# Writing zeros to hold back two weight transfers in the opening of a hybrid layer

## The chip, the cores and the metric

The kernel runs on one core of a Trainium2 chip. The metric is the device time of one execution in microseconds (us); the figure for a kernel is the median of its runs. Engines are named as in the profile: PE is TensorE (PEld its weight loads), DVE is VectorE, ACT is ScalarE, POOL is GpSimd, SP is SyncE, which only issues transfers here. ACTq and SPq are the instruction queues of ScalarE and SyncE; a row there is the issue of a transfer.

## The reference

One layer (`DEPTH = 1`) of a streaming encoder on 256 tokens of width 2048, in float32:

```python
def reference(x, attn_norm, w_in, b_forget, q_norm, k_norm, out_norm_fox, out_norm_sb,
              w_out, ffn_norm, w_up, conv_w, conv_b, w_down):
    for layer in range(DEPTH):
        h = rms_norm(x, attn_norm[layer])
        x = x + hybrid_mixer(h, w_in[layer], b_forget[layer], q_norm[layer], k_norm[layer],
                             out_norm_fox[layer], out_norm_sb[layer], w_out[layer])
        h = rms_norm(x, ffn_norm[layer])
        x = x + conv_ffn(h, w_up[layer], conv_w[layer], conv_b[layer], w_down[layer])
    return x
```

`hybrid_mixer` projects `h @ w_in` (2048 x 6152), splits the columns into queries, keys and values of eight heads of a softmax attention with forget gates and eight heads of a stick-breaking attention, normalizes each group's output and multiplies by `w_out`. `conv_ffn` projects up to 11264 columns, convolves three tokens per channel, gates with SiLU and projects down. The change touches only the first of all these products: the first 512 columns of `h @ w_in`, which are the queries of four heads.

## The kernel before

Every product is made of three: the weights, which arrive as float32 in a buffer `w_raw`, are split into a rounded part `w_hi` (a cast) and the rest `w_lo` (a subtraction), and the activations likewise into the two parts of `hT`. TensorE multiplies hi by hi, lo by hi and hi by lo (L225 to L232, L254 to L266 and, in the opening, L420 to L428).

The first group of columns has a routine of its own, `opening()` (L382 to L471). Inside it the order of TensorE, VectorE, ScalarE and SyncE is the order of the program, written out by hand (`manual_schedule`, L473); GpSimd and everything after the opening, up to the feed-forward part, are put in order by a scheduler that goes by priorities and by its own estimate of times. The feed-forward part is again ordered by hand.

What the opening does, in order:

- The weights' rows 0 to 2047 of the first 512 columns come as eight pieces of 256 rows, called c = 0 to 7; `raws[c]` is half of a `w_raw` buffer of 128 x 2048, so that c = 0 and c = 1 share the first buffer. `load_w(c, which, queue)` issues the transfer of a whole piece (512 KB), or of one of its two halves of 128 rows (256 KB, 512 columns of the buffer). Counted in halves: piece 0 (c = 0, half 0, buffer columns 0 to 511) is issued by SyncE, piece 1 (c = 0, half 1, columns 512 to 1023) and piece 2 (c = 1, half 0, columns 1024 to 1535) by ScalarE, piece 3 (c = 1, half 1, columns 1536 to 2047) by SyncE, as are all pieces after.
- The tokens `x` come in slices of 256 or 512 columns (`load_x`, L91), issued by SyncE between the pieces, L430 to L445. ScalarE issues `prow`, the norm's gains, before its two pieces (L431), and loads its table of functions (L432).
- `keep_busy(n)` (L376) makes TensorE multiply a tile `zeros` by itself n times, into a bank that nobody reads. `zeros` is written by VectorE (L368) before the opening. Fourteen such products stand at TensorE's start, four more before the first real product.
- `columns(ga, ...)` transposes `prow` on TensorE (L128) and VectorE copies it to `ga` (L129). It needs `ident`, which GpSimd writes (L369, L370).
- `split_w(0)` casts piece 0 on VectorE (L406), has the first two columns of blocks of `x` transposed (`ps_x`, L138), scaled by `ga` into `hT` by ScalarE (L143) and VectorE (L146), casts piece 1 on ScalarE (L415) and subtracts both on VectorE (L416). `split_w(1)` casts pieces 2 and 3 on VectorE (L412). Later pieces are cast by ScalarE.
- `multiply` (L420) then makes the products: for c = 0 the eight on `w_hi` (L456, L457), then `behind(0)` (the transposes for c = 1), then the four on `w_lo`; from c = 1 on the transposes for the next c come first, so the transposes that take the slice `load_x(4, 2)` stand between the products of c = 0 and those of c = 1.

Where two instructions touch the same bytes of a buffer, the program is given a wait from the one on the other; two writers of the same bytes are kept in order too.

Of the kernel before, what the change touches and what calls it, by code (L numbers as in the profile page):

```python
# [45 lines left out]
def hybrid_layer(  # L46
# [20 lines left out]
    act, dve = nc.scalar, nc.vector  # L67
# [10 lines left out]
    def f32(t):  # L78
        return t.bitcast(F32)
# [10 lines left out]
    def load_x(k, n):  # L90
        nc.sync.dma_start(x2[:, :, k * P : (k + n) * P], xp[:, :, k * P : (k + n) * P])  # L91
# [34 lines left out]
    def columns(dst, rows, n):  # L126
        pp = psb.tile([P, 512], F32, name="pp", tag="t")
        nc.tensor.transpose(pp[:, :n], rows, ident[:n, :n])  # L128
        dve.tensor_copy(dst, pp[:, :n])  # L129
# [3 lines left out]
    def transposed_split(k, g, n=2):  # L133

        ps = psb.tile([P, 2, S], F32, name="ps_x", tag="t")
        for j in range(n):
            for t in range(NT):
                nc.tensor.transpose(  # L138
                    ps[:, j, t * P : (t + 1) * P], xt[t][:, (k + j) * P : (k + j + 1) * P], ident
                )  # L140
        for j in range(n):
            i = k + j
            act.activation(hT[:, i, 0, :], ps[:, j, :], AF.Identity, scale=g[:, i : i + 1])  # L143
        for j in range(n):
            i = k + j
            dve.scalar_tensor_tensor(  # L146
                hT[:, i, 1, :], ps[:, j, :], g[:, i : i + 1], f32(hT[:, i, 0, :]),
                op0=ALU.mult, op1=ALU.subtract,
            )

    def sums_of_squares(ss, c, tiles=range(NT)):

        for t in tiles:
            junk = late.tile([P, 512], F32, name="junk", tag="raw", bufs=4)
            act.activation(junk, xt[t][:, c * 512 : (c + 1) * 512], AF.Square, accum_out=ss[:, t, c : c + 1])
# [62 lines left out]
    def rows_of(w, k0, n, c0, cols):  # L218
        return w[k0 * P : (k0 + n) * P, c0 : c0 + cols].rearrange("(k p) c -> p k c", p=P)
# [14 lines left out]
    def of_half(h, part, t):  # L234
        return h[:, part, t * P : (t + 1) * P]
# [48 lines left out]
    with ExitStack() as actx:  # L284
# [80 lines left out]


        zeros = at.tile([P, S], mybir.dt.bfloat16, name="zeros")
        dve.memset(zeros, 0.0)  # L368
        nc.gpsimd.memset(ident, 0.0)  # L369
        nc.gpsimd.affine_select(  # L370
            ident, ident, pattern=[[-1, P]], base=0, channel_multiplier=1,
# [4 lines left out]
        def keep_busy(n):  # L376
            for _ in range(n):
                nc.tensor.matmul(idle, zeros[:, :P], zeros, start=True, stop=True)
# [3 lines left out]
        def opening():  # L382

            acc = psa.tile([P, NT, 512], F32, name="acc", tag="acc")
            pairs = [[(0, 1), (1, 1)]] + [[(0, 2)]] * 7
            raws, parts = [], []

            def load_w(c, which=None, queue=nc.sync):

                if c == len(raws):  # L390
                    raw = wraw.tile([P, 2048], F32, name="w_raw", tag="w_raw")
                    raws.extend([raw[:, :1024], raw[:, 1024:]])
                for i, n in [(which, 1)] if which is not None else [(0, 2)]:
                    queue.dma_start(
                        raws[c][:, i * 512 : (i + n) * 512].rearrange("p (a b) -> p a b", a=n),
                        rows_of(wi, 2 * c + i, n, 0, 512),
                    )

            def split_w(c):
                hi = whi.tile([P, 2048], F32R, name="w_hi", tag="w_hi")  # L400
                lo = wlo.tile([P, 2048], F32R, name="w_lo", tag="w_lo")
                parts.append([t[:, :1024].rearrange("p (a b) -> p a b", a=2) for t in (hi, lo)])
                for i, n in pairs[c]:
                    cols = slice(i * 512, (i + n) * 512)
                    if c == i == 0:
                        dve.tensor_copy(hi[:, cols], raws[c][:, cols])  # L406
                        for k in range(2):
                            transposed_split(k, ga, 1)
                    elif c == 1:
                        for j in range(2):  # L410
                            half = slice(512 * j, 512 * (j + 1))
                            dve.tensor_copy(hi[:, half], raws[c][:, half])  # L412
                        transposed_split(2, ga)
                    else:
                        act.copy(hi[:, cols], raws[c][:, cols])  # L415
                    dve.tensor_tensor(  # L416
                        lo[:, cols], raws[c][:, cols], f32(hi[:, cols]), op=ALU.subtract
                    )

            def multiply(c, i, n, high):  # L420
                hi, lo = (p[:, i : i + n] for p in parts[c])
                order = [(j, l, hi) for j in range(n) for l in range(2)] if high else [(j, 0, lo) for j in range(n)]
                for m, (j, l, r) in enumerate(order):
                    for t in range(NT):
                        nc.tensor.matmul(
                            acc[:, t, :], of_half(hT[:, 2 * c + i + j], l, t), r[:, j, :],
                            start=high and c == i == m == 0, stop=not high and c == 7 and m == n - 1,
                        )  # L428

            load_x(0, 2)  # L430
            nc.scalar.dma_start(prow[:KT, :], attn_norm[0].rearrange("(n p) -> n p", p=P))  # L431
            act.preload_act_table_set("natural_log_exp_and_others")  # L432
            load_w(0, 0)
            load_w(0, 1, nc.scalar)
            load_x(2, 2)
            load_w(1, 0, nc.scalar)
            load_w(1, 1)
            load_x(4, 2)
            load_w(2)
            load_x(6, 2)  # L440
            load_w(3)
            load_x(8, 4)
            load_w(4)
            load_x(12, 4)
            load_w(5)  # L445
            keep_busy(14)
            columns(ga, prow[:KT, :], KT)
            split_w(0)
            keep_busy(4)

            def behind(c):
                if c:
                    transposed_split(2 * c + 2, ga)
                split_w(c + 1)

            multiply(0, 0, 1, True)  # L456
            multiply(0, 1, 1, True)  # L457
            behind(0)
            sums_of_squares(ss1, 0, [0])
            multiply(0, 0, 1, False)  # L460
            multiply(0, 1, 1, False)
            for c in range(1, 8):
                if c < 7:
                    behind(c)
                sums_of_squares(ss1, c // 2, [c % 2])
                if c == 2:
                    load_w(6)
                    load_w(7)
                multiply(c, 0, 2, True)
                multiply(c, 0, 2, False)  # L470
            return acc  # L471

        with tc.high_priority(offset=AHEAD), tc.manual_schedule(  # L473
            engines={mybir.EngineType.PE, mybir.EngineType.DVE, mybir.EngineType.Activation, mybir.EngineType.SP}
        ):
            acc_q0 = opening()
# [689 lines left out]
```

## Time and profile before

| | |
|---|---|
| median of 3 runs | 1105.16 us |
| lowest and highest run | 1104.26 and 1108.11 us |
| the profiled execution's own time | 1104.34 us |
| its span, first to last instruction | 1102.6 us |
| TensorE busy | 1097.7 us (100%) |
| VectorE, ScalarE, GpSimd busy | 876.6, 701.1, 44.4 us |
| first product of zeros on TensorE | 1.06 us |
| first real product (L425) | 5.94 us |
| ScalarE issues its two pieces (L394) | from 1.26 us, 0.94 us for both |

Times in the profile count from the first instruction. A row has the start, the length, the engine, the line, the operation, what it writes and reads, and in brackets how long its engine sat idle before it and what ended that. Products are pipelined: a row of several is as long as from the first's start to the last's end, and each is longer than the distance to the next.

### The profile page before, as it was taken

Reading aid. Unit: us, or ns where it says so; the run is one execution under the profiler, and the core shown is the slowest. Engines: PE = TensorE matmul, PEld = TensorE weight load, DVE = VectorE, ACT = ScalarE, POOL = GpSimd, SP = SyncE. Lnnn points to the kernel's source line nnn. Section 1 sums busy time; section 2 is a strip of 40 time slices with the busy share of each in tenths; the row PEclk is TensorE's granted clock in tenths of the full one; section 3 lists DMA queues with packets and bytes.
Section 4 is the critical chain, followed back from the end, with each engine's and each line's share of the span. In section 5 each row is a group of like instructions: output and inputs, shape, how many; then the busy total and the mean of one; then the engine's idle time right before and its main releaser. Section 6 shows DMA issues by size and latency. Waiting matters only on the chain. (4 is left out here: it accounts for less than half of the span.)

```text
span 1102.6 us, 14841 instructions
## 1 busy us (share of the span) xinstructions
PE 1097.7 (100%) x5868; PEld 951.0 (86%) x5868; DVE 876.6 (80%) x941; ACT 701.1 (64%) x879; POOL 44.4 (4%) x46
## 2 busy tenths in 40 slices
PE   9999999999999999999999999999999999999998
PEld 7998888888888888888888888888888888888887
DVE  6656787785775677679889988889798989889896
ACT  6544565664553567667767776767676777677753
POOL 0000000000000000000000010100000010100010
PEclk9999999999999999999999999999999999999999
DMA  8776555565555396558989597987979688997985
GB/s 288 187 230 230 188 153 165 176 216 181 180 165 185 108 323 202 189 172 212 285 228 306 191 238 261 263 268 178 319 206 298 222 220 276 247 266 196 325 212 166
DMA packets 179408, 245.89 MB, mean 223 GB/s; under 512 B 4433, under 2 KB 119019, under 8 KB 179083
## 3 DMA queue, kind: packets, MB, share of 16 engines
q1 hardware_dynamic: 162458, 209.67, 58.2%
q0 software_dynamic: 16560, 34.75, 16.7%
q8 instruction: 46, 0.75, 0.3%
q10 hardware_dynamic: 320, 0.53, 0.1%
q14 instruction: 24, 0.19, 0.0%
HBM read 242.82 MB, written 2.11 MB: 222 GB/s over the span
## 5 line engine op out<-in xcount | busy, mean ns | idle before, releaser
L208 DVE TENSOR_TENSOR w_lo<-w_raw,w_hi 128x2048 fp32r<-128x2048 f32 (+1 forms) x196 | 439.5, 2246 | 148.4 <-ACT w_hi L207 147.5
L207 ACT CAST w_hi<-w_raw 128x2048 fp32r<-128x2048 f32 (+1 forms) x196 | 367.2, 1876 | 273.3 <-PE pu L256 81.7
L256 PE MATMUL pu<-hT,w_hi 128*128 128x512 f32 x1664 | 397.1, 390 | 0.0
L256 PEld LDWEIGHTS pu<-hT,w_hi 128*128 128x128 f32 x1664 | 309.4, 188 | 62.4
L263 PEld LDWEIGHTS pu<-hT,w_lo 128*128 128x128 f32 x1664 | 213.6, 191 | 8.2
L263 PE MATMUL pu<-hT,w_lo 128*128 128x256 f32 x1664 | 216.2, 283 | 0.0
L229 PE MATMUL acc<-w_hi,hT 128*128 128x512 f32 (+1 forms) x576 | 124.9, 368 | 0.0
L229 PEld LDWEIGHTS acc<-w_hi,hT 128*128 128x128 f32 x576 | 101.2, 188 | 14.1
L207 ACT CAST w_hi<-w_sum 128x2048 fp32r<-128x2048 f32 x30 | 57.3, 1909 | 43.0 <-PE pu L256 37.0
L208 DVE TENSOR_TENSOR w_lo<-w_sum,w_hi 128x2048 fp32r<-128x2048 f32 x30 | 68.7, 2289 | 19.6 <-ACT w_hi L207 19.6
L866 ACT ACTIVATE tap<-up,ccol 128x256 f32<-128x256 f32 x176 | 74.6, 495 | 0.0
L229 PE MATMUL acc<-w_lo,hT 128*128 128x512 f32 (+1 forms) x288 | 65.0, 367 | 0.0
L229 PEld LDWEIGHTS acc<-w_lo,hT 128*128 128x128 f32 x288 | 51.5, 188 | 7.4
L971 POOL DMA_DIRECT2D w_sum<-in_w_down_dram x20 | 25.7, 1284 | 796.6 <-DVE w_lo L208 786.1
L229 PE MATMUL acc<-w_hi,oT 128*128 128x512 f32 x192 | 46.0, 392 | 0.0
L229 PEld LDWEIGHTS acc<-w_hi,oT 128*128 128x128 f32 x192 | 35.7, 188 | 7.3
L229 PE MATMUL bank_a<-w_hi,s 128*128 128x512 f32 x160 | 40.1, 393 | 0.2 <-ACT w_hi L207 0.2
L229 PE MATMUL bank_b<-w_hi,s 128*128 128x512 f32 x160 | 40.0, 392 | 0.0
L229 PE MATMUL bank_a<-w_hi,g 128*128 128x512 f32 x160 | 40.0, 392 | 0.0
L229 PEld LDWEIGHTS bank_a<-w_hi,s 128*128 128x128 f32 x160 | 28.8, 189 | 5.8 <-issue 0.6
L229 PEld LDWEIGHTS bank_b<-w_hi,s 128*128 128x128 f32 x160 | 28.9, 189 | 5.3
L229 PEld LDWEIGHTS bank_a<-w_hi,g 128*128 128x128 f32 x160 | 28.9, 189 | 5.2
(211 smaller groups left out, 1070.4 us busy)
## 6 DMA issues: line engine op xcount, KB each, us to landing
w_raw<-in_w_up_dram SPq DMA_DIRECT2D x88, 1024.0 KB, 7.8
w_raw<-in_w_down_dram SPq DMA_DIRECT2D x44, 1024.0 KB, 6.4
w_raw<-in_w_in_dram SPq DMA_DIRECT2D x36, 1024.0 KB, 5.4
w_sum<-in_w_down_dram POOLq DMA_DIRECT2D x20, 1024.0 KB, 10.4
w_raw<-in_w_out_dram SPq DMA_DIRECT2D x16, 1024.0 KB, 5.1
w_raw<-in_w_down_dram POOLq DMA_DIRECT2D x10, 1024.0 KB, 14.5
w_raw<-in_w_in_dram SPq DMA_DIRECT2D x12, 688.0 KB, 4.1
w_raw<-in_w_in_dram SPq DMA_DIRECT2D x6, 512.0 KB, 7.0
```

The source lines that it names most:

```text
L207: act.copy(hi[:, :n], raw[:, :n])
L208: dve.tensor_tensor(lo[:, :n], raw[:, :n], f32(hi[:, :n]), op=ALU.subtract)
L229: nc.tensor.matmul(o, lhs(i, l, t), r[:, i, :], start=starts and j == 0, stop=stops and j == 3 * n - 1, skip_group_check=more,)
L256: nc.tensor.matmul(acc[:, j, :], hi[:, i, j * P : (j + 1) * P], hT[:, k].rearrange("p a b -> p (a b)"), start=k == 0, stop=False,)
L263: nc.tensor.matmul(acc[:, j, S:], lo[:, i, j * P : (j + 1) * P], hT[:, k, 0, :], start=False, stop=k == KT - 1,)
L866: act.activation(taps[w][:, j, :], u[:, j, w : w + S], AF.Copy, scale=ccol[:, w, f : f + 1])
L971: nc.gpsimd.dma_start(mem[into][:, : nk * 512].rearrange("p (a b) -> p a b", a=nk), src, accum_op=ALU.add)
```

## The change

The write of `zeros` moves to the head of the opening. The first `w_raw` buffer is remembered (`firsts`), and after SyncE's transfer of piece 0 is in the program VectorE writes zeros to columns 512 to 1535 of that buffer, the places of pieces 1 and 2. ScalarE's two transfers write the same bytes, so they now wait until VectorE is done. The products of zeros become 12 and 2 in place of 14 and 4.

```diff
@@ -365,7 +365,6 @@
         zeros = at.tile([P, S], mybir.dt.bfloat16, name="zeros")
-        dve.memset(zeros, 0.0)
         nc.gpsimd.memset(ident, 0.0)
...
@@ -383,12 +382,14 @@
             acc = psa.tile([P, NT, 512], F32, name="acc", tag="acc")
             pairs = [[(0, 1), (1, 1)]] + [[(0, 2)]] * 7
-            raws, parts = [], []
+            raws, parts, firsts = [], [], []
+            dve.memset(zeros, 0.0)
 
             def load_w(c, which=None, queue=nc.sync):
 
                 if c == len(raws):
                     raw = wraw.tile([P, 2048], F32, name="w_raw", tag="w_raw")
+                    firsts.append(raw)
                     raws.extend([raw[:, :1024], raw[:, 1024:]])
...
@@ -431,6 +432,7 @@
             nc.scalar.dma_start(prow[:KT, :], attn_norm[0].rearrange("(n p) -> n p", p=P))
             act.preload_act_table_set("natural_log_exp_and_others")
             load_w(0, 0)
+            dve.memset(firsts[0][:, 512:1536], 0.0)
             load_w(0, 1, nc.scalar)
             load_x(2, 2)
             load_w(1, 0, nc.scalar)
@@ -443,10 +445,10 @@
             load_w(4)
             load_x(12, 4)
             load_w(5)
-            keep_busy(14)
+            keep_busy(12)
             columns(ga, prow[:KT, :], KT)
             split_w(0)
-            keep_busy(4)
+            keep_busy(2)
```

## The prediction, made before the change was run

> **What bounds the kernel now.** I read the page's head first, then the waits of TensorE over the whole span, then the order of time of the first 10 us, where all of the change lies.
>
> ```profile
> span 1102.6 us, 14841 instructions
> ...
> PE 1097.7 (100%) x5868; PEld 951.0 (86%) x5868; DVE 876.6 (80%) x941; ACT 701.1 (64%) x879; POOL 44.4 (4%) x46
> ```
>
> ```profile
> PE idle L378 <- DVE zeros L368: 1.1, 1, 1.1
> PE acc L425 <- ACT hT L143: 0.3, 1, 0.3
> PE bank_a L229 <- ACT w_hi L207: 0.2, 1, 0.2
> ```
>
> TensorE is busy for all but 1102.6 - 1097.7 = 4.9 us. Its three waits are 1.1 us before the first product of zeros, 0.3 us before the first real product, and 0.2 us much later; the other 3.3 us lie behind its last product, as the end of the order of time shows:
>
> ```profile
> 1098.65 0.64 PE L1044 MATMUL bank_a<-w_lo,g 128*128 128x256 f32 x4
> 1099.32 0.42 DVE L948 TENSOR_TENSOR x<-x,bank_a 128x256 f32<-128x256 f32 x1 [1.01 <-PE bank_a L1044]
> ```
>
> So from the first real product to 1099.3 us TensorE is the kernel. What the change can move is when this unbroken run begins, and whether a hole opens in it. Either passes to the end one for one.
>
> These are the rows of the opening, in order of time (start, length, engine, line). Of merged rows only the first instruction starts at the time given; SPq and ACTq rows are transfers being issued, not moved.
>
> ```profile
> 0.73 0.46 ACTq L431 DMA_DIRECT2D prow<-in_attn_norm_dram  x1
> 0.83 0.17 DVE L368 MEMSET zeros<- 128x128 uint32 x1 [0.83 <-PEq L1151]
> 1.06 3.17 PE L378 MATMUL idle<-zeros 128*128 128x256 bf16 x14 [1.06 <-DVE zeros L368]
> 1.23 1.28 ACT L432 ACT_TABLE_LOAD   x1 [1.23 <-PEq L1151]
> 1.23 0.46 SPq L394 DMA_DIRECT2D w_raw<-in_w_in_dram  x1
> 1.26 0.94 ACTq L394 DMA_DIRECT2D w_raw<-in_w_in_dram  x2
> 2.73 0.65 SPq L91 DMA_DIRECT2D x<-in_x_dram  x1
> 3.75 0.38 SPq L394 DMA_DIRECT2D w_raw<-in_w_in_dram  x1
> 4.16 0.28 PE L128 MATMUL pp<-cs,prow 16*128 16x16 f32 x1
> 4.37 0.81 PE L138 MATMUL ps_x<-cs,x 128*128 128x128 f32 x4
> 4.48 0.17 DVE L129 COPY ga<-pp 128x16 f32<-128x16 f32 x1 [3.48 <-PE pp L128]
> 5.00 0.84 ACT L143 ACTIVATE hT<-ps_x,ga 128x256 fp32r<-128x256 f32 x2 [2.49 <-PE ps_x L138]
> 5.02 0.60 PE L378 MATMUL idle<-zeros 128*128 128x256 bf16 x4
> 5.37 0.43 DVE L406 CAST w_hi<-w_raw 128x512 fp32r<-128x512 f32 x1 [0.72 <-DMA w_raw<-in_w_in_dram]
> 5.73 0.62 ACT L415 CAST w_hi<-w_raw 128x512 fp32r<-128x512 f32 x1
> 5.94 2.08 PE L425 MATMUL acc<-w_hi,hT 128*128 128x512 f32 x8 [0.32 <-ACT hT L143]
> 7.70 0.42 DVE L412 CAST w_hi<-w_raw 128x512 fp32r<-128x512 f32 x1
> 8.22 1.18 PE L425 MATMUL acc<-w_lo,hT 128*128 128x512 f32 x4
> 8.41 0.43 DVE L412 CAST w_hi<-w_raw 128x512 fp32r<-128x512 f32 x1 [0.30 <-DMA w_raw<-in_w_in_dram]
> 9.19 0.42 PEld L138 LDWEIGHTS ps_x<-cs,x 128*128 128x128 f32 x4 [0.23 <-issue]
> 9.24 0.61 PE L138 MATMUL ps_x<-cs,x 128*128 128x128 f32 x4
> 9.61 2.07 PE L425 MATMUL acc<-w_hi,hT 128*128 128x512 f32 x8
> ```
>
> Three points are to be seen. The first real product, at 5.94, follows the cast of weight piece 0, done at 5.37 + 0.43 = 5.80, and ScalarE's second `hT`, done at 5.00 + 0.84 = 5.84; the wait is put down to the second, but both end within 0.04 us. The cast began when its transfer landed. Then pieces 1 to 3 of the weights follow with hardly a wait: piece 1 (a ScalarE transfer) is cast at 5.73 with no idle before it, piece 2 (ScalarE's other) at 7.70 with none, piece 3 at 8.41 after 0.30 us on its transfer. And the third group of transposes, at 9.24, takes the slice of `x` that was issued at 2.73. Its weight load sat idle for 0.23 us with nothing shown to hold it, although weight loads elsewhere run ahead of the products. I read this as that transfer landing about 9.1: `x` arrives just as TensorE gets there.
>
> **The change part by part.** *The write of zeros.* It is a VectorE memset of 128 x 1024 words behind the one at 0.83. No such size is in the trace; the nearest rows are these.
>
> ```profile
> L368 DVE MEMSET zeros<- 128x128 uint32 x1 | 0.2, 165 | 0.8 <-PEq L1151 0.8
> ...
> L822 DVE MEMSET up<- 128x4 f32 x2 | 0.1, 62 | 0.0
> ...
> 10.17 1.22 DVE L416 TENSOR_TENSOR w_lo<-w_raw,w_hi 128x1024 fp32r<-128x1024 f32 x1
> ```
>
> 124 more words cost 103 ns, 0.83 ns each, so 1024 cost 62 + 1020 x 0.83 = 0.91 us. Below stand two 128x512 casts, 2 x 0.43 = 0.86; above stands the subtraction of the same width, 1.22. I take 0.91, since it comes from memsets. The zeros then end at 1.00 + 0.91 = 1.91 us (1.86 to 2.22). VectorE has no work until 4.48, so its 3.48 us of waiting hide this, and the first products of zeros need only the first memset. The Trainium skill, "VectorE: DVE Perf Modes", section "Zero memsets can be issued as uint32 (trn2)", has a memset at one cycle per element; at its 0.96 GHz an estimate is 1.07 us, which would move the end of the zeros to 2.07 and the sum by under 0.2 us. The slope of 0.83 ns between the two rows is below that rule, and two rows can't settle it.
>
> *The wait.* ScalarE's two transfers move from 1.26 to 1.91 (up to 2.22), 0.65 to 0.96 us later. Behind them in ScalarE's queue stands only `hT` at 5.00; both are issued 0.94 us later, by 3.2 at worst, so 1.8 us hide that. The table load stands ahead and is not moved. SyncE's order is unchanged, but its later transfers wait for earlier ones to land, so I looked whether it is held up: its next 512 KB are issued from 3.75 on, while this slice of `x` is already out at 2.73. GpSimd waits for none of this.
>
> Who gains: piece 0. The queues' bytes up to 4.0 and up to 4.5 us (q1 is SyncE's, q10 ScalarE's):
>
> ```profile
> q1 hardware_dynamic: 353, 0.43, 38.7%
> q10 hardware_dynamic: 72, 0.09, 6.6%
> ...
> q1 hardware_dynamic: 398, 0.50, 38.8%
> q10 hardware_dynamic: 131, 0.21, 13.0%
> ```
>
> Piece 0 and the `x` ahead of it are 2 x 256 KB, 0.52 MB, so at 4.5 piece 0 had hardly 0.02 MB left, and ScalarE's queue had passed 0.21 MB. Held back 0.65 us, ScalarE's queue would have passed at 4.5 about what it had at 3.85, under 0.09 MB: 0.12 MB less, which at (0.71 - 0.52)/0.5 = 0.38 MB per us is 0.3 us. Piece 0 comes up to 0.3 us earlier and the first real product starts at 5.6 to 5.9.
>
> Who loses: piece 1. It had landed by 5.73; 0.65 later is 6.38, its cast ends at 7.00. The eight first products, 2.08 us with the last one 0.39 us long, stand 0.24 us apart, so the fifth, the first on piece 1, began at 5.94 + 4 x 0.24 = 6.9. Now it begins at 7.05: 0.15 late, 0.45 at the other end (0.96 later), and not late at all if piece 1 loses only part of the delay. Piece 2 becomes 8.4 instead of 7.7; its place is taken by piece 3, which is not behind it any more, and both casts end at 8.8 to 9.0, before the products that need them at 9.61. No loss.
>
> Who sets the end: the slice of `x` at 9.1. Every byte ahead of it is still ahead of it, only in another order, so it lands when it did. A start 0.3 us earlier is therefore waited off at 9.24, and a delay of 0.15 is passed on. The term is -0.05 to +0.45 us; I take +0.1.
>
> *Fewer products of zeros.* Fourteen took 3.17 us with 0.42 the last one, 0.21 us apart; two fewer let the transpose of `prow` go at 3.85 instead of 4.16, for `prow` itself lands about 3.7 (SyncE's issue at 3.75 was released by it):
>
> ```profile
> SPq L394 <- DMA prow<-in_attn_norm_dram: 0.4, 1, 0.4
> ```
>
> `ga` and `hT` can then be up to 0.3 us earlier. This only lets the first product follow piece 0, and is inside the term above. The two products dropped at 5.02 lay in a stretch in which TensorE waited anyway: nothing, unless the clock minds.
>
> The sum: the profiled execution took 1104.34 us, 1.74 beyond its span and 0.82 below the median of the three runs, 1105.16. 1104.34 + 0.1 = 1104.4, and on the median 1105.2 to 1105.3. I forecast 1105.2, no change. A change of 0.3%, 3.3 us, is about what a measurement of this kernel can tell from none.
>
> **The rivals.** *The clock stays slow (slower).* The first thirteen products of zeros are all at the long length, the four at 5.02 at the short one:
>
> ```profile
> L378 PE MATMUL idle<-zeros x13: 395/421/422, 1.1 to 3.6; 128*128 128x256 bf16 x13
> ...
> L378 PE MATMUL idle<-zeros x4: 273/273/273, 5.0 to 5.3; 128*128 128x256 bf16 x4
> ```
>
> Their spacing falls from 0.21 to (0.60 - 0.27)/3 = 0.11 us: TensorE doubled its speed between 3.6 and 5.02, 2.5 to 4 us into unbroken work, while the granted clock reads full throughout. The change tears holes of some 0.3 us at 3.6 and 0.6 us before the first product. If these cost it one more such interval, real products run at half speed from 5.9 until about 8 to 9.6: a loss of 1.0 to 1.8 us, with no slack at 9.24 to hide it, so 1106.6 on the median. It decides if the doubling comes after 5.9. For it: TensorE must have been at work for most of an interval. Against: the holes are 0.9 of 4.5 us. The Trainium skill, "TensorE: Matmul & The Clock Gate", Part 1, says that a free-running window of about 3.4 us of activity releases the clock, not a count of products; the trace agrees as to the size. By its figure one more window at half speed would be 1.7 us, an estimate.
>
> *The zeros wait for piece 0 (slower).* Zeros and piece 0 lie in one buffer. If the order were kept by buffer, VectorE could write only from 5.37, ScalarE would issue at 6.3 instead of 1.26, and at the 4.1 us from issue to landing that piece 0 had, piece 1 would land at 10.4, be cast by 11.05, and the fifth product would start 4.2 us late: 1109.4. Against: in the rows above piece 1 goes out at 1.26, 0.03 us behind piece 0, into the same buffer, without a wait. It decides as soon as the zeros end after 2.2.
>
> ```profile
> w_raw<-in_w_in_dram SPq DMA_DIRECT2D x1, 256.0 KB, 4.1
> ```
>
> *The early start is kept (faster).* If `x` at 9.1 comes earlier too, the whole 0.3 us is kept: 1104.9. More isn't there: a gain of 3.3 us would need two thirds of all of TensorE's 4.9 idle us, most of which lie at the end.
>
> *The wait does nothing.* If ScalarE's queue is slow to begin anyhow (0.09 MB by 4.0), piece 1 is hardly later: 1105.1, not to be told from the forecast.
>
> **How the numbers follow.** No change in the sense of the sum, with the wait that does nothing: 0.75. The clock stays slow: 0.10. The early start is kept: 0.05. Zeros behind piece 0: 0.04. What is left, 0.06, is that a program order after the opening comes out differently, for which I have no row; I give it 0.04 slower and 0.02 faster by over 0.3%. So faster 0.03 (with 0.01 for runs that scatter), slower 0.09 (0.04 + 0.04 + 0.01), same 0.88. The range: below, the lowest run shown, 1104.26, less the 0.3 kept and a little, 1103.8; above, the slow clock's 1106.6 and a third of the 2.95 us by which the highest run, 1108.11, lies over the median, 1107.6.
>
> **What would show it.** Right: the two ACTq rows at L394 near 1.9 to 2.2; VectorE's cast at L406 before 5.37; the first product between 5.6 and 5.9; ScalarE's cast at L415 after 6.0; the transposes at 9.24 within 0.2 us of there; no new wait of TensorE later. Wrong: products at L425 some 0.43 us apart after 6 us (the clock), the long memset starting at 5.4 (the buffer), or the third transposes clearly before 9.0 or after 9.7.

## The result: slower by about 0.3%

| | before | changed |
|---|---|---|
| median | 1104.51 us (22 runs) | 1108.66 us (22 runs) |
| lowest and highest run | 1104.15, 1108.11 | 1105.74, 1113.37 |
| profiled execution's own time | 1104.34 us | 1110.44 us |

The ratio is 1.0032, with a 95% interval of [1.0026, 1.0038]. The forecast was 1105.2 us, in a range from 1103.8 to 1107.6; it stood on a median of three runs, 1105.16, which 22 runs put at 1104.51. The runs of the changed kernel fall in two groups: 6 of the 22 lie between 1105.74 and 1106.54, the other 16 from 1107.37 up. In the kernel before, 19 of 22 lie within 0.4 us of the median.

The head of the page of the changed kernel, and the waits of TensorE over its span:

```profile
span 1108.7 us, 14834 instructions
...
PE 1101.0 (99%) x5864; PEld 952.9 (86%) x5864; DVE 877.8 (79%) x942; ACT 701.4 (63%) x879; POOL 44.4 (4%) x46
```

```profile
PE bank_a L229 <- ACT w_hi L207: 2.4, 1, 2.4
PE idle L377 <- DVE zeros L386: 1.1, 1, 1.1
PE acc L426 <- ACT w_hi L416: 0.7, 1, 0.7
PE acc L426 <- ACT hT L143: 0.2, 1, 0.2
```

TensorE is *busy* 3.3 us longer with four products fewer, and has a new wait of 0.7 us on ScalarE's cast of piece 1. The order of time of the opening shows both (from L394 on the line numbers are one or two higher here; the products of zeros are now L377, and the write of `zeros` L386):

```profile
1.06 2.74 PE L377 MATMUL idle<-zeros 128*128 128x256 bf16 x12 [1.06 <-DVE zeros L386]
1.16 0.91 DVE L435 MEMSET w_raw<- 128x1024 f32 x1 [0.16 <-issue]
2.11 0.87 ACTq L395 DMA_DIRECT2D w_raw<-in_w_in_dram  x2
3.73 0.28 PE L128 MATMUL pp<-cs,prow 16*128 16x16 f32 x1
4.02 1.11 PE L138 MATMUL ps_x<-cs,x 128*128 128x128 f32 x4
5.22 0.43 DVE L407 CAST w_hi<-w_raw 128x512 fp32r<-128x512 f32 x1 [0.99 <-DMA w_raw<-in_w_in_dram]
5.79 2.04 PE L426 MATMUL acc<-w_hi,hT 128*128 128x512 f32 x4 [0.23 <-ACT hT L143]
7.85 0.62 ACT L416 CAST w_hi<-w_raw 128x512 fp32r<-128x512 f32 x1 [2.20 <-DMA w_raw<-in_w_in_dram]
8.52 2.07 PE L426 MATMUL acc<-w_hi,hT 128*128 128x512 f32 x4 [0.69 <-ACT w_hi L416]
11.10 2.05 PE L426 MATMUL acc<-w_lo,hT 128*128 128x512 f32 x4
13.56 2.09 PE L426 MATMUL acc<-w_hi,hT 128*128 128x512 f32 x8
```

Two things have happened. Piece 1, issued 0.85 us later, landed at 7.85 in place of 5.73 at the latest, so its products start at 8.52 in place of 6.9. And four products now take as long as eight did: until 13.5 us TensorE runs at half speed. The record of the granted clock in this trace begins only at 13.46 us; before the change it begins at 4.74. The products' own lengths say the same, in the changed kernel (first) and before; the columns are count, shortest, median and longest in ns:

```profile
L426 PE MATMUL acc<-w_hi,hT x8: 628/628/793, 5.8 to 10.0; 128*128 128x512 f32 x8
...
L425 PE MATMUL acc<-w_hi,hT x16: 389/393/476, 5.9 to 11.3; 128*128 128x512 f32 x16
```

The products of the second pair of blocks begin at 13.56; before, they began at 9.61. That is 3.95 us, and the same distance stands near the end of the span (the changed kernel first):

```profile
1077.94 3.79 PE L1046 MATMUL acc<-w_hi,g 128*128 128x512 f32 x16
...
1074.02 3.79 PE L1044 MATMUL acc<-w_hi,g 128*128 128x512 f32 x16
```

So 3.92 us of the loss are made in the first 13.5 us and then carried along. The remaining 2.2 us of the 6.1 between the two spans is the wait of 2.4 us at `bank_a`, at 1086 us, on a late transfer of the last weights; it was 0.2 before. This wait came out between 0 and 1.5 us in the profiles of the other kernels below, so runs can differ by that much for a reason that lies far behind the opening. It makes this one profile worse than the median, and whether the change has a part in it is left open.

### The profile page after: what moved, and what is told of

Its sections match the earlier page's. It is cut to its first block, busy times and chain, and to the rows that moved or that the text cites. A ratio compares the mean times of both kernels' runs of the same rounds, so it can differ in the third digit from the quotient of the medians.

```text
span 1108.7 us, 14834 instructions
## 1 busy us (share of the span) xinstructions
PE 1101.0 (99%) x5864; PEld 952.9 (86%) x5864; DVE 877.8 (79%) x942; ACT 701.4 (63%) x879; POOL 44.4 (4%) x46
## 3 DMA queue, kind: packets, MB, share of 16 engines
HBM read 242.82 MB, written 2.11 MB: 221 GB/s over the span
```

## The experiments

Two theories stood against each other. *Transfer*: what costs is that piece 1 comes late. *Clock*: what costs is that TensorE's clock comes up late, and the late piece only adds a hole. All times are medians, with the kernel before measured beside them on the same chip. There are eleven runs of each, twelve of e13. (e9 to e11 gave no time; e12 to e14 are the same edits again.)

| | edit against | time (lowest to highest) | before beside it | ratio |
|---|---|---|---|---|
| e1 | changed, 14 and 4 products | 1106.15 (1105.29 to 1106.33) | 1104.69 | 1.0011 [1.0003, 1.0020] |
| e2 | before, 12 and 2 products | 1106.11 (1104.25 to 1107.06) | 1104.69 | 1.0010 [1.0002, 1.0019] |
| e3 | changed, hole filled, 14 and 6 | 1106.27 (1105.40 to 1106.60) | 1104.69 | 1.0014 [1.0005, 1.0023] |
| e4 | changed, half the zeros, 14 and 4 | 1105.01 (1104.01 to 1106.99) | 1104.69 | 1.0003 [0.9993, 1.0012] |
| e5 | changed, again | 1106.21 (1105.68 to 1108.79) | 1104.59 | 1.0019 [1.0010, 1.0028] |
| e6 | before, 6 and 0 products | 1107.45 (1105.84 to 1108.07) | 1104.59 | 1.0022 [1.0013, 1.0031] |
| e7 | e1, and SyncE held back too | 1105.43 (1105.13 to 1105.76) | 1104.59 | 1.0009 [1.0000, 1.0018] |
| e8 | changed, hole filled, 12 and 2 | 1106.47 (1105.69 to 1107.72) | 1104.59 | 1.0018 [1.0009, 1.0027] |
| e12 | e1, zeros written elsewhere | 1105.38 (1104.79 to 1106.99) | 1105.02 | 1.0002 [0.9993, 1.0010] |
| e13 | before, 12 and 4 products | 1105.95 (1104.58 to 1110.76) | 1105.02 | 1.0017 [1.0005, 1.0029] |
| e14 | before, 14 and 2 products | 1105.71 (1104.86 to 1108.99) | 1105.02 | 1.0007 [0.9998, 1.0016] |

**The two parts alone.** e1 is the wait without the fewer products:

```diff
-            keep_busy(12)
+            keep_busy(14)
...
-            keep_busy(2)
+            keep_busy(4)
```

> The changed kernel with the products of zeros put back to 14 and 4; the wait stays. In the profile of the changed kernel piece 1 landed at 7.83 us (5.59 before), and the clock record begins at 13.5 us (4.7 before), with the products some 0.43 us apart until then. Theory 'clock': the missing products of zeros keep the clock slow. Then here the clock is up before the first product, and only the late piece 1 is left: its four products start at 8.5 in place of 6.95, 1.6 us, so 1106.1 with little scatter. Theory 'transfer': the hole that the late piece 1 tears in TensorE's work is what keeps the clock slow, however many products of zeros stand ahead: as the changed kernel, 1108 to 1109 in most runs.

e2 makes the opposite edit of the same two lines in the kernel before.

> The kernel before with 12 and 2 products of zeros; no zeros are written and nothing waits. Theory 'clock': the holes of 0.3 us at 3.7 and 0.6 us before the first product already delay the clock in at least some runs, by one interval of about 3.4 us at half speed: 1105.5 to 1106.3 in those. Theory 'transfer': piece 1 is in time, there is no large hole, the clock comes before 6 us: 1104.5, within 0.3 of the kernel before.

e3 puts 14 products of zeros into the hole before piece 1, and has 14 and 6 elsewhere:

```diff
             multiply(0, 0, 1, True)
+            keep_busy(14)
             multiply(0, 1, 1, True)
```

> The changed kernel with 14 and 6 products of zeros and 14 more between the products of piece 0 and those of piece 1, so that TensorE has no hole while it waits for piece 1. Both theories agree that the clock then comes early; it measures the transfer's price alone. If piece 1 lands at 7.8 as in the changed kernel, its products start at 8.5 in place of 6.95: 1.6 us, 1106.1, runs within 0.5 us of each other. If it is still at 1108 and more, neither theory holds.

In e1, in order of time, the real products go at full speed again (four in 1.19 us), and only the late piece 1 is left:

```profile
7.80 0.62 ACT L416 CAST w_hi<-w_raw 128x512 fp32r<-128x512 f32 x1 [1.81 <-DMA w_raw<-in_w_in_dram]
8.48 1.19 PE L426 MATMUL acc<-w_hi,hT 128*128 128x512 f32 x4 [1.02 <-ACT w_hi L416]
```

Its 1.46 us over the kernel before are what the clock theory had for it, and e3 measures the same price, 1.58 us, with all but 0.4 us of the hole filled (piece 1 was cast at 8.39 in its profile); both keep their runs within 1.2 us. So a late piece 1 costs some 1.5 us when the clock is up before its products.

e2, where nothing is late, costs 1.42 us in the median, but its runs spread over 2.8 us. Its one profile, of a run of 1105.16, has the clock up at 4.92, before the first product, and starts the second pair of blocks at 9.60, as early as before. What this run has over the profile before, 0.8 us, is the wait at `bank_a`, 1.0 us in place of 0.2:

```profile
9.60 2.09 PE L425 MATMUL acc<-w_hi,hT 128*128 128x512 f32 x8
...
PE bank_a L229 <- ACT w_hi L207: 1.0, 1, 1.0
```

So the profile doesn't show that the clock cost e2 anything. A wait at `bank_a` that varies is a rival for the spread of its runs, and no run here separates the two. Only one of the eleven, at 1106.11, has a mean granted clock below 0.999.

**The clock by itself.** e6 is the larger dose:

```diff
-            keep_busy(14)
+            keep_busy(6)
...
-            keep_busy(4)
```

> The kernel before with 6 products of zeros at the start and none behind: no zeros are written, nothing waits, piece 1 lands at 5.6. A larger dose of the one suspected cost. If the fewer products cost through the clock, the profile shows the first products on piece 0 some 0.43 us apart and the clock record beginning at 7.5 to 10 us, and the time is 1106.5 to 1107. If the 1.4 us of the kernel with 12 and 2 had another cause (an order, the end of the span), this one gives no more than 1105.

```profile
5.82 0.62 ACT L415 CAST w_hi<-w_raw 128x512 fp32r<-128x512 f32 x1
...
6.18 3.72 PE L425 MATMUL acc<-w_hi,hT 128*128 128x512 f32 x8 [0.98 <-DVE w_hi L406]
9.74 0.60 PE L138 MATMUL ps_x<-cs,x 128*128 128x128 f32 x4
10.09 1.17 PE L425 MATMUL acc<-w_lo,hT 128*128 128x512 f32 x4
```

No transfer is held back here, but the first eight products take 3.72 us in place of 2.08, and from 9.7 on everything is at full speed. The second pair of blocks begins at 11.46 in place of 9.61: 1.85 us, from the clock and from the later start at 6.18. This run, of 1106.26, is the second fastest of its eleven; what the others lost beyond that, up to the median's 2.86 us, no profile shows. e13 and e14 take the two reductions apart:

> The kernel before with 12 products of zeros at the start in place of 14, and the four behind kept. Theory 'clock': both reductions make holes, this one 0.3 us between the last product of zeros and the transposes; if the early hole is the one that counts, 1105.5 to 1106.1 with the scatter of the kernel with 12 and 2; if it is not, 1104.6. The transposes start some 0.3 us earlier, so the four behind end earlier too, and the hole before the first product grows to about 0.7 us.

> The kernel before with 14 products of zeros at the start and two behind in place of four: the hole before the first real product grows by 0.22 us, to about 0.55, and nothing else moves. If the late hole alone can cost a run its early clock, 1105 to 1106 in some runs; if a hole of that size is forgiven, 1104.6 with the scatter of the kernel before.

Each alone leaves most runs as they were and throws a few far up: four of e13's twelve are at 1109.11 to 1110.76, two of e14's eleven at 1108.77 and 1108.99, and these six are the only ones whose mean granted clock is 0.998; the rest have 0.999 or 1.000. The kernel before does it too, once in 29 runs beside them (1108.30, 0.998), and not once in the 66 beside the other kernels. So neither reduction is always forgiven. The interval of e14 still touches 1, so for it the two runs are the evidence and not the median: its profiled run, which is the median one, begins the second pair of blocks at 9.68, only 0.07 us late, and loses its time in a wait of 1.5 us at `bank_a`.

How the six runs lost so much is not shown, for none of them was profiled. An estimate: 3.4 us at half clock cost at most 1.7 us and take 0.5 x 3.4 / 1105 = 0.0015 off the mean clock, which is what these runs show; they lie 3.7 to 5.7 us above the kernel before. The mean leaves out what lies before a clock record begins, so a clock that also came late would not be seen in it.

**Both together.** e5 is the changed kernel itself.

> The changed kernel once more, beside the next three and on their chip. So far: the wait alone (14 and 4 products of zeros) cost 1.5 us, the fewer products alone 1.4, both together 4.15 in the first measurement. Theory 'sum': the two prices are independent, and the first measurement lay high: 1107.6. Theory 'together': with fewer products the clock is not yet up when the hole before piece 1 comes, and the hole then keeps it down for one interval of 3.4 us more: 1108.5 again, and the clock record of the profile begins near 10 or 13.5 us.

e8 fills the hole before piece 1, with the edit of e3 and 12 and 2 products.

> The changed kernel, with 12 and 2 products of zeros as in the change, and 14 more between the products of piece 0 and those of piece 1, so that the hole there is filled. Theory 'together' (the hole keeps a clock down that is not up yet): the filling takes away what the two cost beyond their sum, 1106.3 to 1107.6, and no run over 1108. Theory 'sum': the filling changes nothing at the clock, as the changed kernel run beside it.

The median of e5 hits neither theory. Nine of its eleven runs lie at 1105.68 to 1106.86, which is the price of the late piece alone, and two at 1108.18 and 1108.79, both with a clock of 0.998. The profile is of the first of these two. Its stretches, cut where the granted clock changes (columns: busy time and count of each engine, granted clock, share and rate of the transfers):

```profile
2.00:4.70 2.70, 2.59 (x13) 1.70 (x12) 0.25 (x2) 0.51 (x1) 0.00 (x0) 1.00 0.87 254
4.70:8.10 3.40, 1.75 (x9) 0.86 (x7) 1.90 (x4) 1.38 (x3) 0.00 (x0) 1.00 1.01 337
8.10:11.50 3.40, 3.27 (x10) 2.68 (x11) 1.45 (x3) 0.38 (x2) 0.00 (x0) 0.50 1.03 367
11.50:13.50 2.00, 2.00 (x12) 1.67 (x11) 1.43 (x3) 1.85 (x6) 0.00 (x0) 0.99 1.04 395
```

The 1.00 of the first row says only that the record has not begun; the twelve products of zeros there stand 0.21 us apart, which is half speed. The clock was up from 4.7, TensorE was busy for 1.75 of the next 3.40 us because piece 1 was missing, and then the clock was halved for the next 3.4 us, just when piece 1 had come. So in this run the clock changed in steps of 3.4 us, and was taken away after one in which TensorE was half idle. The Trainium skill, "TensorE: Matmul & The Clock Gate", Part 1, describes such a free-running window of about 3.4 us; these stretches agree with its length. Where it warns, under "HAM oscillation — how this bites in real kernels", of idle gaps above some 3.4 us, the measurement differs: here the hole was 1.6 us long, and TensorE was half busy in the window.

That missing products of zeros can also keep the clock from coming is seen when the first profile of the changed kernel is laid beside that of e1. Counted back from 13.46 in steps of 3.41 us, the intervals of the first end at 6.63 and 10.05; e1's clock record begins at 6.62, so the two runs stand almost alike. In the interval up to there e1 was busy for all 3.41 us, and the clock came. The changed kernel, four products of zeros short, was busy for 3.17 us, and it did not come; nor did it after the next interval, with 2.73 us, but only after one without a hole. Once up, e1's clock stayed through an interval with 2.39 us of work. Busy time alone is no rule for its coming, though: e14 got the clock after an interval with 2.67 us, idle until the first product of zeros at 1.06, and what makes the difference is not shown.

The profile of the changed kernel in the section on the result is of the rarer kind. Of the 16 runs from 1107.37 up 11 have a mean clock of 0.998, like e5's two; the profiled one has 1.000, because what it lost lies before its record.

e8 has no run over 1107.72, as "together" expected, but its median is 0.26 above that of e5, whose runs mostly had the clock, and in its profile 0.8 us of the hole were left. With eleven runs of each, that the filling helps is suggested, not shown. How often a run loses its clock was 16 of 22 in the first measurement (taking the runs from 1107.37 up) and 2 of 11 in e5. What sets this share is not settled. The place of the intervals is the likeliest candidate: where the clock came at the first chance, its record begins anywhere from 3.73 us (e14) to 6.62 (e1), although the products of zeros begin at 1.06 in every profile. The chip may be another.

**Why 0.85 us became 2.1.** In e4 the zeros cover piece 1 alone, with 14 and 4 products:

```diff
-            dve.memset(firsts[0][:, 512:1536], 0.0)
+            dve.memset(firsts[0][:, 512:1024], 0.0)
```

> The changed kernel with 14 and 4 products of zeros, and zeros written to the place of piece 1 alone (512 columns in place of 1024), so ScalarE can issue at about 1.65 in place of 2.11 us. If a transfer is served in the order in which it was issued on either queue, it is now ahead of SyncE's slice of x at 1.74 (at 2.11 it was behind it): its data begins some 1.65 us after the issue, as before, it lands at about 6.0, its products are not late and the time is 1104.6. If the lateness just grows with the delay (2.2 us for 0.85), it lands at 6.5: 1104.8 with the clock up, and a hole of 0.3 us.

In e7 VectorE also holds back a transfer of SyncE, again with 14 and 4:

```diff
             dve.memset(firsts[0][:, 512:1536], 0.0)
+            dve.memset(x2[:, :, 2 * P : 4 * P], 0.0)
```

> The changed kernel with 14 and 4 products of zeros, and VectorE also writes zeros to the slice of x that SyncE issues third, behind the zeros for pieces 1 and 2. So SyncE's third to fifth transfers are held back as well, to about 2.65 us, and ScalarE's two at 2.1 are ahead of them again, as in the kernel before. Theory 'order': piece 1 was 2.2 us late for a delay of 0.85 because SyncE's transfers got ahead of it. Then it lands some 4.4 us after its issue, at 6.5, the hole before its products is under 0.4 us, and the time is 1104.9 to 1105.4, with the fourth and fifth transfers of SyncE up to 0.9 us later. Theory 'share': two queues share alike whatever was issued first, and a late start is simply slow: it lands at 7.8 again, 1106.2 or more.

In e4 ScalarE issued at 1.57, 0.31 us later than before, and cast piece 1 at 6.29, between the two expectations; the time can't be told from that of the kernel before. So it decides nothing between them. e7 does more. These are the bytes that each queue had moved by 5.0 us (q1 SyncE, q10 ScalarE) before, in the changed kernel and in e7:

```profile
q1 hardware_dynamic: 478, 0.59, 40.2%
q10 hardware_dynamic: 175, 0.27, 15.7%
...
q1 hardware_dynamic: 600, 0.71, 47.9%
q10 hardware_dynamic: 44, 0.03, 2.7%
...
q1 hardware_dynamic: 461, 0.54, 33.2%
q10 hardware_dynamic: 144, 0.22, 27.3%
```

`prow` and piece 1 are 0.27 MB. Before, ScalarE's queue had moved that much at 5.0. In the changed kernel it had hardly begun, 2.9 us after its issue at 2.11; in e1, e3, e5 and e8, with the same wait, it had moved 0.05 MB. In e7 it issued at the same time and had moved 0.22 MB, because SyncE's next slice of `x` went out at 2.64 and not at 1.74. Its cast of piece 1 stands between the two:

```profile
2.64 0.41 SPq L91 DMA_DIRECT2D x<-in_x_dram  x1
...
7.12 0.62 ACT L416 CAST w_hi<-w_raw 128x512 fp32r<-128x512 f32 x1 [1.13 <-DMA w_raw<-in_w_in_dram]
```

So a good part of the extra lateness is that SyncE's transfers got ahead, and e7 gives back 0.6 us of the price: 0.84 us over the kernel before in place of 1.46. Not all of it, since piece 1 still needed 5.0 us from issue to cast, against 4.5 before. (SyncE also sent two small parameter transfers ahead of that slice in e7, at 1.74 and 2.21.)

**The writing itself.** e12 writes the zeros to a tile of its own:

```diff
-            dve.memset(firsts[0][:, 512:1536], 0.0)
+            spare = at.tile([P, 1024], F32, name="spare")
+            dve.memset(spare, 0.0)
```

> The changed kernel with 14 and 4 products of zeros, and the 1024 columns of zeros written to a tile that nothing else uses: VectorE does the same work at the same place, but no transfer waits for it. If the writing itself cost anything (VectorE's time, or a port that the transfers into the same memory need), piece 0 or the first product would be later than before. I expect nothing: 1104.6, both transfers issued from 1.26, piece 1 landed by 5.7.

```profile
1.16 0.91 DVE L436 MEMSET spare<- 128x1024 f32 x1 [0.16 <-issue]
1.25 0.94 ACTq L395 DMA_DIRECT2D w_raw<-in_w_in_dram  x2
6.00 0.62 ACT L416 CAST w_hi<-w_raw 128x512 fp32r<-128x512 f32 x1
```

The transfers go out at 1.25 again, and the time can't be told from the kernel before beside it. The write costs nothing that these runs can tell (at most 1.1 us by the interval); the wait does. No experiment points to a version that beats the kernel before.

## Why the prediction was wrong

- **What bounds the kernel**: right. 3.95 us lost in the opening are 3.92 us at 1078 us. Only the wait at `bank_a` behind that, 0.2 us before and 0 to 2.4 in the other kernels, was not reckoned with.
- **The write of zeros**: right, 0.91 us as worked out from the two memsets. It began 0.16 us later than assumed, at 1.16, so it ended at 2.07 and ScalarE issued at 2.11, inside the bounds of 1.86 to 2.22, though these allowed for the length and not for the start. The zeros did not wait for piece 0, so that rival is out.
- **Who gains**: right in kind. Piece 0 was cast at 5.22 in place of 5.37, half of what was forecast; over the profiles it is more, 4.74 to 5.37 in the five with this wait and SyncE's order as it was, 5.37 to 5.75 in the six without a wait. The reading behind it was wrong: SyncE's queue stood at 0.59 MB at 5.0, beyond the 0.52 of piece 0 and the `x` ahead of it, and piece 0 was still not cast until 5.37, so bytes of later transfers were among them.
- **Who loses: this step failed.** "0.65 later is 6.38" moved the landing by as much as the issue. An issue 0.85 late made piece 1 land at least 2.1 late, in good part because the place in the order of transfers was lost with it (e7); the rest of the lateness stays open. The term was put at -0.05 to +0.45 us; e1 and e3 measure 1.5. The paragraph before it had ScalarE's queue 0.12 MB poorer at 4.5 and gave the gain to piece 0, but nothing asked when piece 1 would catch up against the transfers that SyncE had issued meanwhile, the slice of `x` at 1.74 above all. The rival that the wait does nothing is out as well.
- **Fewer products of zeros: this step failed too, in chance and in size.** "Nothing, unless the clock minds" priced the holes at zero and gave the clock 0.10. The mechanism was named rightly, and its sign in the profile, products 0.43 us apart after 6 us, is there. The holes came out smaller than the 0.3 and 0.6 us that it counted with: `prow` was there earlier, so its transpose followed the products of zeros at once, at 3.73, and TensorE waited 0.2 us before the first product. Even so the clock did not come at 6.6 in the changed kernel, where it came in e1, and each reduction alone has runs with a lower mean clock (e13, e14). The price of 1.0 to 1.8 us took it as lost for one interval only. With piece 1 late it can be lost for two intervals, or be granted and taken away again; most runs above 1108 are 2 to 3 us over those with the late piece alone.
- **Adding up**: the rivals were priced one at a time. Here the late piece makes a hole (1.6 us in e5's profile), and a hole was the very thing that decides the clock rival. The late piece and the late clock had to be one case.
- **Who sets the end**: the third transposes, expected within 0.2 us of 9.24, came at 12.95; the slice of `x` no longer set anything.

## What to carry to other kernels

A transfer that is held back can lose its place as well as the delay: before shifting it, look at what the other queues will have issued by then, and price its landing behind those bytes. Products of zeros at a start are there for the clock, so a hole that costs nothing by the waits can still cost the clock. The only figures here are intervals of 3.4 us: 2.39 us of work kept it (e1), 1.75 lost it (e5), and 3.17 did not bring it (the changed kernel). And when one edit makes a hole and another weakens what keeps the clock, price them together, and look at the spread of the runs: two groups were the sign of the clock here.

## What was not expected of the hardware

The granted clock fell from 1.00 to 0.50 for 3.4 us after a stretch in which TensorE was still busy for half the time (1.75 of 3.40 us). An interval in which it was busy for 3.17 of 3.41 us did not bring the clock up where one without a hole did. And a transfer issued by ScalarE at 2.11 us had moved almost nothing by 5.0 (0.03 MB with `prow`'s own bytes), while one issued at the same time with SyncE's next slice held back had moved 0.22 MB.
